# Two layers with a mixture of experts on one core: four chunks of the first expert loaded into other rooms, and another order of the experts

## The chip, the cores and the metric

The kernel runs on one core of a Trainium2 chip. The metric is the device time of one execution in microseconds, as the median over several executions. Before the change it is 1270.76 us (three runs, 1269.85 to 1271.94).

## The reference

The input x has 256 tokens (two blocks of 128) of 1024 channels, in float32. Two layers follow. Each has a token mixer made of four groups (a convolution, a pooling mixer, two kinds of attention), with one projection in (1024 to 2304) and one out (1024 to 1024). The first layer then has a dense SwiGLU of inner width 2816. The second has eight SwiGLU experts of inner width 3584, and each token goes to the two with the highest router values:

```
logits = t @ router
top_vals, top_idx = lax.top_k(logits, 2)
gates = softmax(top_vals)
combine = sum(one_hot(top_idx, 8) * gates[..., None], axis=1)
for e in range(8):
    y = y + combine[:, e:e+1] * ((silu(t @ wg[e]) * (t @ wu[e])) @ wd[e])
```

A last RMSNorm ends it. All weights are float32, and nearly all of their bytes belong to the experts.

## The kernel before

**Chunks.** The host lays all weights out as 395 chunks of 128 partitions by 2048 float32, 1 MB each (`_stream`): 13 for the mixer of layer 0, 33 for the dense network, 13 for the mixer of layer 1 (59 so far), and then 336 for the experts, 42 each. An expert is worked in seven slabs of 512 inner columns. A slab has six chunks: two for the gate, two for the up and two for the down projection. Chunk number k of an expert is numbered as they lie in memory; the kernel asks for them in the order gate and up of slab s, then down of slab s-1.

**The ring.** A chunk is loaded by `chunk` (L135; the load itself is L148), always from the queue of the engine SP, into a room of 8 KB per partition that `raw` (L125) hands out. Up to the mixer of layer 1 there are nine rooms. When that mixer's own tiles are given back, eight more rooms are laid in their place (L663), so that the experts have 17. A room is free again when the last instruction that reads it is done. The first loads of the experts are chained with `issue_after` (L147), which keeps them in program order on SP.

**High and low parts.** Where the full 128 rows of a block are multiplied, the weights are first split in two: `halves` (L167) makes, for each half of a chunk, a tile `hi` on ScalarE (L179) and a tile `lo` on VectorE (L180), 1024 elements per partition each, with four rooms for `hi` and four for `lo` (two chunks). Each product is then three matmuls (`moving`, L196).

**Wide and narrow experts.** The tokens of an expert are gathered by a one-hot matmul (`gather`, L937), turned (`gathered_T`, L947), multiplied by gate and up (`gate_or_up`, L973; the products are L208 for a wide and L991 for a narrow expert), turned again (`act_T`, L1002), multiplied by down (`down`, L1018; L208 or L1036) and scattered back (`scatter`, L1043; matmuls L1055, additions to x L1056). A wide expert has place for 128 tokens and uses the high and low parts. A narrow one has place for 64: it multiplies the chunk in float32 as it was loaded, two chains of 64 columns side by side, and doesn't touch `hi` and `lo`.

**The order of the experts.** Expert 0 comes first and is narrow; its chunks have addresses that are known when the kernel is built. The other seven are ranked by their number of tokens while the kernel runs. SP reads the seven ranks into registers (`values_load`, L1075, one after the other), because the addresses of their chunks depend on them. Ranks 0 to 2 are wide and ranks 3 to 6 narrow, and they are taken in the order of `TURNS` (L56):

```
TURNS = (0, 3, 1, 4, 2, 5, 6)
...
turns = turns + [Turn(ranked_c[r], pos_r, comb_r, r, r < WIDE) for r in TURNS]
```

So the sequence is narrow (expert 0), wide, narrow, wide, narrow, wide, narrow, narrow. Below, N0 is expert 0, N3 to N6 are the narrow ones by rank, and W0 to W2 the wide ones.

**What sets the order of each queue.** In the program text, the reading of the ranks stands ahead of all chunk loads of the experts. The stretch of the router runs under `manual_schedule`, which fixes the order on ScalarE, VectorE, GpSimd and TensorE. Everything else, SP's queue too, is laid out by the framework's planner when the kernel is built: it goes through the program by its own estimates of when operands and rooms are there, and may pull a load ahead of instructions that stand before it. On the chip each engine then takes its queue strictly in this order, and an instruction that waits holds back all that stands behind it.

Of the kernel before, what the change touches and what calls it, by code (L numbers as in the profile page):

```python
# [10 lines left out]
F32 = mybir.dt.float32  # L11
# [9 lines left out]
P = 128  # L21
# [21 lines left out]
RING = 9  # L43
RING2 = 8
LATE = 3
HALVES = 4
# [6 lines left out]


WIDE = 3
TURNS = (0, 3, 1, 4, 2, 5, 6)  # L56
NARROW = P // 2


# [34 lines left out]
def trunk(ctx: ExitStack, tc: tile.TileContext, x_in, wst, cst, par_a, par_l, gains, out):  # L94
    nc = tc.nc
# [4 lines left out]
    hi_p = ctx.enter_context(tc.tile_pool(name="hip", bufs=HALVES))  # L100
    lo_p = ctx.enter_context(tc.tile_pool(name="lop", bufs=HALVES))
# [12 lines left out]
    HF = [slice(0, 512), slice(512, 1024)]  # L114
# [8 lines left out]
    loaded = []  # L123

    def raw():  # L125
        turn[0] += 1
        return ring[(turn[0] - 1) % len(ring)].tile([P, CH], F32, name="raw")

    def gain(n, dst=None):

        g = raw()[:, :D] if dst is None else dst
        nc.sync.dma_start(g, bass.AP(tensor=gains.tensor, offset=gains.offset + n * D, ap=[[0, P], [1, D]]))
        return g

    def chunk(c, src=None, split=False):  # L135

        r = raw()
        src = wst[c] if src is None else src
        if c == 0 or split:
            for j in range(2):  # L140
                nc.sync.dma_start(r[:, j * 1024:(j + 1) * 1024], src[:, j * 1024:(j + 1) * 1024])
            if c == 0:
                nc.sync.dma_start(x[:, 1], x_in[P:, :])
        else:
            with ExitStack() as st:
                if c is not None and MOE0 < c < MOE0 + RING + RING2:
                    st.enter_context(tc.issue_after(loaded.pop()))  # L147
                loaded[:] = [nc.sync.dma_start(r, src).ins]  # L148
        return r
# [17 lines left out]
    def halves(c, on_pool=(), between=lambda: None):  # L167

        r = chunk(c) if isinstance(c, int) else c
        res = []  # L170
        for j in range(2):
            w = r[:, j * 1024:(j + 1) * 1024]
            hi = hi_p.tile([P, 1024], F32R, name="hi")
            lo = lo_p.tile([P, 1024], F32R, name="lo")
            eng = nc.gpsimd if j in on_pool else nc.vector
            with ExitStack() as st:
                for ins in behind if split[0] >= FIRST else ():
                    st.enter_context(tc.issue_after(ins))
                nc.scalar.activation(hi, w, AF.Copy)  # L179
                eng.tensor_tensor(out=lo, in0=w, in1=hi.bitcast(F32), op=SUB)  # L180
            split[0] += 1
            if split[0] == HALVES:
                behind.clear()
            res.append((hi, lo))
            if j == 0:
                between()
        return res
# [8 lines left out]
    def moving(ps, xx, w):  # L196

        return (ps, xx[0], w[0]), (ps, xx[1], w[0]), (ps, xx[0], w[1])
# [5 lines left out]
    def products(items, start=False, stop=False):  # L204

        seq = [m for it in items for m in it]
        for n, (ps, lhs, rhs) in enumerate(seq):
            nc.tensor.matmul(ps, lhs, rhs, start=start and all(m[0] is not ps for m in seq[:n]),  # L208
                             stop=stop and all(m[0] is not ps for m in seq[n + 1:]))

    def cut(pair, *at):
        return tuple(w[at] for w in pair)
# [510 lines left out]
    def moe(c0, before):  # L723
        with ExitStack() as st:
# [187 lines left out]
            class Turn:  # L912
# [5 lines left out]
                def chunk(self, k, split):  # L918
                    c = self.c + k
                    if isinstance(c, int):  # L920
                        return chunk(c, None, split)
                    return chunk(None, wst[bass.ds(c, 1)].rearrange("o p c -> (o p) c"), split)

            def experts(turns, oh=None):

                OH, XT, OT, HT, DP, adds, later = {}, {}, {}, {}, {}, {}, []
# [4 lines left out]
                ROWS = [slice(0, NARROW), slice(NARROW, P)]  # L931
# [41 lines left out]
                def gate_or_up(i, which):  # L973

                    e, s = divmod(i, NSLAB)
                    ps = acc.tile([P, 512], F32, name="acc")
                    for j in range(2):  # L980
                        r = turns[e].chunk(6 * s + 2 * which + j, False)
                        if turns[e].wide:
                            hs = halves(r)
                            for q in range(2):
                                w = tuple(h.rearrange("p (k c) -> p k c", k=2) for h in hs[q])
                                products([moving(ps, cut(XT[e], ALL, 4 * j + 2 * q + k), cut(w, ALL, k)) for k in range(2)],
                                         j + q == 0, j + q == 2)
                        else:
                            w = r.rearrange("p (k c) -> p k c", k=4)
                            for k in range(4):  # L990
                                nc.tensor.matmul(ps[ROWS[k % 2]], XT[e][:, 4 * j + k], w[:, k],  # L991
                                                 start=j == 0 and k < 2, stop=j == 1 and k > 1)
                        if later and j:
                            later.pop(0)()
                    return ps
# [22 lines left out]
                def down(i, between=()):  # L1018
                    e, s = divmod(i, NSLAB)
                    if s == 0:  # L1020
                        DP[e] = [sc.tile([P, 512], F32, name="sc") for n in range(2)]
                    for j in range(2):
                        r = turns[e].chunk(6 * s + 4 + j, i == NE * NSLAB - 1 and j == 1)
                        if turns[e].wide:
                            hs = halves(r)
                            order = [(n, hf) for n in range(2) for hf in range(2)]
                            if i == NE * NSLAB - 1 and j == 1:

                                order.sort(key=lambda o: o[1])
                            products([moving(DP[e][hf], cut(HT[i], ALL, 2 * j + n), cut(hs[n], ALL, HF[hf])) for n, hf in order],  # L1030
                                     s + j == 0, s == NSLAB - 1 and j == 1)
                        else:
                            w = r.rearrange("p (n d) -> p n d", n=2)
                            for hf in range(2):
                                for n in range(2):
                                    nc.tensor.matmul(DP[e][hf][ROWS[n]], HT[i][:, 2 * j + n], w[:, n, HF[hf]],  # L1036
                                                     start=s + j == 0, stop=s == NSLAB - 1 and j == 1)
                        for f in between if j == 0 else ():
                            f()
                    if s == NSLAB - 1:  # L1040
                        scatter(e)

                def scatter(e):  # L1043
                    ys = []
                    for hf in range(2):
                        yh = wk.tile([P, 512], F32R, name="yh", tag="hmh", bufs=2)
                        yl = wk.tile([P, 512], F32R, name="yl", tag="hml", bufs=2)
                        part(yh, yl, DP[e][hf])
                        ys.append((yh, yl))

                    def add(hf, t):
                        cc = HF[hf]
                        ps = acc.tile([P, 512], F32, name="acc") if e == NE - 1 else tr.tile([P, 512], F32, name="tr")
                        for n, y in enumerate(ys[hf]):
                            nc.tensor.matmul(ps, OT[e][:, t], y, start=n == 0, stop=n == 1)  # L1055
                        nc.vector.scalar_tensor_tensor(x[:, t, cc], ps, turns[e].weight[:, t, turns[e].col:turns[e].col + 1],  # L1056
                                                       x[:, t, cc], op0=MUL, op1=ADD)

                    for hf in range(2):
                        for t in range(NT):  # L1060
                            adds[t, hf] = lambda t=t, hf=hf: add(hf, t)
                    if e < NE - 1:
                        later.extend(adds.values())
# [8 lines left out]
                if oh is not None:  # L1072
                    weights()
                    for r in range(NE - 1):
                        v = nc.values_load(rank_i[0:1, r:r + 1], engines=[mybir.EngineType.SP], min_val=0, max_val=NE - 1)  # L1075
                        ranked_c.append(v * ECH + MOE0)
                    turns = turns + [Turn(ranked_c[r], pos_r, comb_r, r, r < WIDE) for r in TURNS]
                for i in range(NE * NSLAB):
                    e, s = divmod(i, NSLAB)
                    wide, lo = turns[e].wide, ROWS[0]  # L1080
# [174 lines left out]
```

## Time and profile before

| | |
|---|---|
| median of three runs | 1270.76 us |
| the profiled execution's own time | 1272.39 us |
| its span, from the first to the last instruction | 1270.5 us |
| mean granted clock of TensorE | 0.988 of full speed |
| TensorE busy in matmuls | 94% of the span |
| VectorE / ScalarE / GpSimd busy | 58% / 47% / 6% |
| read from the device's memory | 419.75 MB |

The profile's times count from the span's first instruction; the execution's own time holds 1.9 us more than the span. `acc`, `sc` and `tr` are accumulators of TensorE, `raw` the rooms of the ring, `wst` the stream of chunks; L208 under TensorE (PE) is a wide expert's product (or one of the mixer's), L991 and L1036 a narrow expert's.

### The profile page before, as it was taken

The page shows a single profiled execution, that of the slowest core. Times are in us where ns is not written, and L with a number is a line of the kernel's source. Part 1 is how long each engine was busy: PE and PEld are TensorE (multiplying, and loading weights), DVE is VectorE, ACT ScalarE, POOL GpSimd, SP SyncE. Part 2 cuts the span into 40 slices and gives each one's busy share as a digit, 9 for nine tenths or more (in the row PEclk, how much of TensorE's full clock was granted, in tenths as well). Part 3 has the DMA queues.
Part 4 walks back from the last instruction along what each step waited for, and adds up shares of the span by engine and source line. Part 5 has one row for each costly group of instructions (what it writes and reads, how often), then busy time and mean ns, then how long its engine had stood idle before and what let it go on. Part 6 is the DMA issues. An engine that isn't in the chain of part 4 may idle for free.

```text
span 1270.5 us, 16628 instructions
## 1 busy us (share of the span) xinstructions
PE 1198.4 (94%) x6154; PEld 791.8 (62%) x6154; DVE 738.0 (58%) x1118; ACT 596.1 (47%) x868; POOL 75.7 (6%) x45
## 2 busy tenths in 40 slices
PE   8789999999979999999999999999999999999975
PEld 6667999998767633588743378873338887333321
DVE  6986655556897521798751288883139886212112
ACT  5464544444556412576731277772137775222211
POOL 2413000001602100000000000000000000000000
PEclk9899999999999999999999999999999999999998
DMA  9523655455343499999999999999999999999994
GB/s 367 229 100 105 227 199 199 168 185 192 145 139 152 197 421 419 421 417 419 420 419 420 420 420 420 419 419 420 419 419 418 420 419 419 415 419 419 420 420 198
DMA packets 59561, 421.96 MB, mean 332 GB/s; under 512 B 6608, under 2 KB 6864, under 8 KB 9168
## 3 DMA queue, kind: packets, MB, share of 16 engines
q1 hardware_dynamic: 59472, 420.82, 81.8%
q8 instruction: 50, 0.82, 0.3%
q14 instruction: 39, 0.32, 0.1%
HBM read 419.75 MB, written 1.05 MB: 331 GB/s over the span
## 4 chain that ended last, share of the span: by engine, by line
PE 50%; DMA 11%; DVE 4%; ACT 2%; issue 1%; POOL 0%; POOLq 0%; SPq 0%; ACTq 0%; DVEq 0%
PE acc L208 17%; PE acc L991 15%; DMA raw<-wst 11%; PE sc L208 8%; PE sc L1036 5%; DVE xs L1000 1%; DVE xs L1094 1%; PE tr L942 1%; ACT xs L999 1%; PE tr L1006 1%; DVE lo L180 1%; PE tr L1055 1%; PE tr L1012 1%; PE tr L961 0%; ACT hi L179 0%
## 5 line engine op out<-in xcount | busy, mean ns | idle before, releaser
L180 DVE TENSOR_TENSOR lo<-raw,hi 128x1024 fp32r<-128x1024 f32 x351 | 419.8, 1240 | 114.7 <-ACT hi L179 110.0
L179 ACT ACTIVATE hi<-raw 128x1024 fp32r<-128x1024 f32 x370 | 374.4, 1055 | 137.7 <-PE acc L208 70.4
L991 PE MATMUL acc<-raw,xt 128*64 128x512 f32 x1120 | 251.3, 595 | 7.0 <-DMA raw<-wst 6.6
L1000 DVE TENSOR_TENSOR xs<-xs,acc 64x512 f32<-64x512 f32 x70 | 48.3, 690 | 277.6 <-ACT xs L999 277.5
L991 PEld LDWEIGHTS acc<-raw,xt 128*64 128x64 f32 x1120 | 77.3, 137 | 164.0 <-issue 143.5
L999 ACT ACTIVATE xs<-acc 64x512 f32<-64x512 f32 x70 | 41.4, 592 | 213.9 <-PE acc L991 213.9
L208 PE MATMUL acc<-lo,xgh 128*128 128x512 f32 x336 | 134.3, 400 | 1.9 <-DVE lo L180 1.6
L1036 PE MATMUL sc<-raw,ht 128*64 128x512 f32 x560 | 132.3, 598 | 2.8 <-ACT xs L999 1.9
L208 PE MATMUL acc<-hi,xgh 128*128 128x512 f32 x336 | 132.8, 395 | 0.0
L208 PE MATMUL acc<-hi,xgl 128*128 128x512 f32 x336 | 132.6, 395 | 0.0
L208 PE MATMUL sc<-hTh,hi 128*128 128x256 f32 x336 | 93.0, 277 | 0.0
L208 PE MATMUL sc<-hTl,hi 128*128 128x256 f32 x336 | 92.9, 277 | 0.0
L208 PE MATMUL sc<-hTh,lo 128*128 128x256 f32 x336 | 92.9, 276 | 0.0
L208 PE MATMUL acc<-lo,hTh 128*128 128x512 f32 (+1 forms) x192 | 71.0, 397 | 13.9 <-DVE lo L180 13.9
L1036 PEld LDWEIGHTS sc<-raw,ht 128*64 128x64 f32 x560 | 38.2, 136 | 72.5 <-issue 69.9
L208 PEld LDWEIGHTS acc<-lo,xgh 128*128 128x128 f32 x336 | 63.2, 188 | 21.3 <-DVE lo L180 6.4
L208 PEld LDWEIGHTS acc<-hi,xgl 128*128 128x128 f32 x336 | 63.2, 188 | 14.8
L208 PEld LDWEIGHTS acc<-hi,xgh 128*128 128x128 f32 x336 | 63.3, 188 | 13.8
L208 PE MATMUL acc<-hi,hTl 128*128 128x512 f32 (+1 forms) x192 | 70.5, 387 | 0.2
L208 PE MATMUL acc<-hi,hTh 128*128 128x512 f32 (+1 forms) x192 | 70.2, 393 | 0.0
L208 PE MATMUL sc<-hi,hmh 128*128 128x512 f32 x168 | 66.6, 396 | 0.0
L208 PE MATMUL sc<-hi,hml 128*128 128x512 f32 x168 | 66.4, 396 | 0.0
(265 smaller groups left out, 1550.3 us busy)
## 6 DMA issues: line engine op xcount, KB each, us to landing
raw<-wst SPq DMA_DIRECT2D x393, 1024.0 KB, 19.8
raw<-gains SPq DMA_DIRECT2D x4, 512.0 KB, 4.7
raw<-wst SPq DMA_DIRECT2D x4, 512.0 KB, 12.5
pl<-par_l SPq DMA_DIRECT2D x2, 803.5 KB, 8.8
out<-raw SPq DMA_DIRECT2D x4, 256.0 KB, 3.8
x<-x_in SPq DMA_DIRECT2D x2, 256.0 KB, 3.2
x<-x_in SPq DMA_DIRECT2D x1, 512.0 KB, 8.2
xs<-gains SPq DMA_DIRECT2D x1, 512.0 KB, 16.2
```

The source lines that it names most:

```text
L179: nc.scalar.activation(hi, w, AF.Copy)
L180: eng.tensor_tensor(out=lo, in0=w, in1=hi.bitcast(F32), op=SUB)
L208: nc.tensor.matmul(ps, lhs, rhs, start=start and all(m[0] is not ps for m in seq[:n]), stop=stop and all(m[0] is not ps for m in seq[n + 1:]))
L942: nc.tensor.matmul(pg[q].rearrange("p k c -> p (k c)"), OH[e][:, t], src[:, t, HF[q]], start=t + n == 0, stop=t + n == 2)
L991: nc.tensor.matmul(ps[ROWS[k % 2]], XT[e][:, 4 * j + k], w[:, k], start=j == 0 and k < 2, stop=j == 1 and k > 1)
L999: nc.scalar.activation(dst[ROWS[0]], ps[ROWS[0]], AF.Copy)
L1000: nc.vector.tensor_add(dst[ROWS[0]], dst[ROWS[0]], ps[ROWS[1]])
L1006: nc.tensor.transpose(ps[:, n, :NARROW], hm[ROWS[0], n * P:(n + 1) * P], ident[ROWS[0], ROWS[0]])
L1012: nc.tensor.transpose(ps[:, n], hm[:, n * P:(n + 1) * P], ident)
L1036: nc.tensor.matmul(DP[e][hf][ROWS[n]], HT[i][:, 2 * j + n], w[:, n, HF[hf]], start=s + j == 0, stop=s == NSLAB - 1 and j == 1)
L1055: nc.tensor.matmul(ps, OT[e][:, t], y, start=n == 0, stop=n == 1)
L1094: nc.vector.tensor_mul(hm[lo], hm[lo], sg[lo])
```

## The change

Three edits. `TURNS` begins with rank 3 instead of rank 0, so that the sequence is N0, N3, W0, W1, N4, W2, N5, N6. For the narrow expert with the known address (expert 0), the chunks with k from 17 to 20 are no longer loaded into the ring by `chunk` but by the new `two_tiles`: each goes as two transfers of 512 KB into one room of `hi` and one of `lo`, chained to the loads before them. In the order in which the program asks for chunks these are the 17th to 19th (k = 18, 19 and 20) and the 22nd (k = 17). And the narrow products take the half of a chunk that they need through `half`, from a chunk in one piece or from the pair of tiles.

```
-TURNS = (0, 3, 1, 4, 2, 5, 6)
+TURNS = (3, 0, 1, 4, 2, 5, 6)
...
+    def two_tiles(c):
+        r = [pool.tile([P, 1024], F32, name=n, tag=n) for pool, n in ((hi_p, "hi"), (lo_p, "lo"))]
+        for j, dst in enumerate(r):
+            with tc.issue_after(loaded.pop()):
+                loaded[:] = [nc.sync.dma_start(dst, wst[c][:, j * 1024:(j + 1) * 1024]).ins]
+        return r
+
+    def half(r, j):
+        return r[j] if isinstance(r, list) else r[:, j * 1024:(j + 1) * 1024]
...
                 def chunk(self, k, split):
                     c = self.c + k
                     if isinstance(c, int):
+                        if not self.wide and 0 <= k - RING - RING2 < HALVES:
+                            return two_tiles(c)
                         return chunk(c, None, split)
...
-                            w = r.rearrange("p (k c) -> p k c", k=4)
                             for k in range(4):
-                                nc.tensor.matmul(ps[ROWS[k % 2]], XT[e][:, 4 * j + k], w[:, k],
+                                w = half(r, k // 2).rearrange("p (k c) -> p k c", k=2)
+                                nc.tensor.matmul(ps[ROWS[k % 2]], XT[e][:, 4 * j + k], w[:, k % 2],
                                                  start=j == 0 and k < 2, stop=j == 1 and k > 1)
...
-                            w = r.rearrange("p (n d) -> p n d", n=2)
                             for hf in range(2):
                                 for n in range(2):
-                                    nc.tensor.matmul(DP[e][hf][ROWS[n]], HT[i][:, 2 * j + n], w[:, n, HF[hf]],
+                                    nc.tensor.matmul(DP[e][hf][ROWS[n]], HT[i][:, 2 * j + n], half(r, n)[:, HF[hf]],
                                                      start=s + j == 0, stop=s == NSLAB - 1 and j == 1)
```

## Rows read from the trace of the kernel before

**Rows 1.** The page: busy time of TensorE over the span, and, in 40 equal slices of the span, the share of TensorE and of the DMA engines in tenths and what the DMA engines moved.

```profile
PE 1198.4 (94%) x6154; PEld 791.8 (62%) x6154; DVE 738.0 (58%) x1118; ACT 596.1 (47%) x868; POOL 75.7 (6%) x45
...
PE   8789999999979999999999999999999999999975
...
DMA  9523655455343499999999999999999999999994
GB/s 367 229 100 105 227 199 199 168 185 192 145 139 152 197 421 419 421 417 419 420 419 420 420 420 420 419 419 420 419 419 418 420 419 419 415 419 419 420 420 198
```

**Rows 2.** Busy times of three stretches around the entry to the experts: us, busy us and instructions of each engine, TensorE's clock, the share of the DMA engines, and GB/s.

```profile
415.00:425.00 10.00, 10.00 (x49) 8.34 (x48) 4.11 (x8) 2.76 (x5) 1.40 (x2) 1.00 0.88 361
425.00:439.50 14.50, 13.39 (x91) 9.23 (x91) 10.48 (x53) 7.20 (x14) 2.11 (x2) 1.00 0.01 1
439.50:1249.50 810.00, 783.21 (x3566) 440.26 (x3564) 423.64 (x459) 371.79 (x480) 0.00 (x0) 1.00 1.01 419
```

**Rows 3.** SP's queue in order of time, 400 to 420 us and 436 to 446 us: start, length, number of loads. It issued nothing between the two.

```profile
402.07 12.64 SPq L148 DMA_DIRECT2D raw<-wst  x8
...
438.84 6.88 SPq L148 DMA_DIRECT2D raw<-wst  x9
```

**Rows 4.** What SP's queue waited for, in 427 to 436 us (first row) and in 1040 to 1100 us (second): us in total, times, the longest.

```profile
SPq L1075 <- DVE by_rank L851: 20.0, 1, 20.0
...
SPq L148 <- DVE lo L180: 27.9, 11, 4.8
```

**Rows 5.** VectorE's last step before the ranks can be read, from the timeline.

```profile
434.44 0.22 DVE L851 TENSOR_TENSOR by_rank<-cs,rf 128x64 bf16<-128x64 f32 x1
```

**Rows 6.** Chunk loads issued from SP: number, size and median us from issue to landing. First from the start to 427 us (two rows: whole chunks, and the first chunk in two pieces), then from 436 to 439 us, from 1075 to 1080 us, and over the whole span (the page).

```profile
raw<-wst SPq DMA_DIRECT2D x71, 1024.0 KB, 4.9
raw<-wst SPq DMA_DIRECT2D x2, 512.0 KB, 7.0
...
raw<-wst SPq DMA_DIRECT2D x1, 1024.0 KB, 4.8
...
raw<-wst SPq DMA_DIRECT2D x2, 1024.0 KB, 10.3
...
raw<-wst SPq DMA_DIRECT2D x393, 1024.0 KB, 19.8
```

**Rows 7.** The chain that ended last, in order of time (start, us, what): the last products of the mixer's projection out, and then the first and last products of the experts. L991 begins a narrow expert, L208 after L1036 begins a wide one, L1036 x24 ends a narrow one. The last two rows are the last load of the stream and the products on it.

```profile
414.93 6.64 PE acc L208 x29
...
422.45 2.75 PE acc L208 x12
...
436.55 10.52 PE acc L991 x48
...
512.90 5.33 PE sc L1036 x24
...
522.13 12.95 PE acc L208 x54
...
628.30 0.02 issue
...
631.18 2.59 PE acc L208 x10
...
646.22 1.87 PE acc L991 x8
...
736.56 12.96 PE acc L208 x54
...
860.74 1.87 PE acc L991 x8
...
951.07 12.99 PE acc L208 x54
...
1075.20 1.87 PE acc L991 x8
...
1231.23 19.84 DMA raw<-wst
...
1251.21 4.38 PE sc L1036 x16
```

**Rows 8.** Busy times by stretch (columns as in rows 2), from the first product of one expert to that of the next: W0, N3, and N5; the last row runs from the first product of N6 to the last.

```profile
522.13:646.22 124.09, 124.00 (x552) 99.52 (x554) 105.80 (x101) 88.85 (x100) 0.00 (x0) 1.00 1.01 419
646.22:736.56 90.34, 85.56 (x399) 30.25 (x399) 24.40 (x37) 23.42 (x41) 0.00 (x0) 1.00 1.01 419
...
1075.20:1161.60 86.40, 83.02 (x394) 28.94 (x393) 19.43 (x28) 19.57 (x36) 0.00 (x0) 1.00 1.01 418
1161.60:1255.59 93.99, 82.69 (x371) 25.89 (x370) 17.95 (x26) 16.08 (x30) 0.00 (x0) 1.00 0.97 400
```

**Rows 9.** VectorE's instructions by group in the stretch of N3 (646 to 736 us), those that hand one expert over to the next: shapes, number, busy us, mean ns, idle time before them.

```profile
L1056 DVE SCALAR_TENSOR_TENSOR x<-tr,comb_r,x 128x512 f32<-128x512 f32 x6 | 4.4, 748 | 3.9 <-PE tr L1055 3.8
L216 DVE TENSOR_TENSOR yl<-sc,yh 128x512 fp32r<-128x512 f32 x4 | 2.7, 689 | 6.2 <-ACT yh L215 6.2
L216 DVE TENSOR_TENSOR xgl<-tr,xgh 128x512 fp32r<-128x512 f32 x2 | 1.3, 686 | 1.8 <-ACT xgh L215 1.8
```

**Rows 10.** TensorE in order of time near the end (start, us, products, and in brackets the idle time before them and what ended it).

```profile
1208.72 1.94 PE L991 MATMUL acc<-raw,xt 128*64 128x512 f32 x8 [1.04 <-DMA raw<-wst]
1211.21 1.94 PE L991 MATMUL acc<-raw,xt 128*64 128x512 f32 x8 [0.56 <-DMA raw<-wst]
```

## The prediction

> **What bounds the kernel now.** Begin with the page's 40 slices [rows 1]: from the fifteenth slice (445 us) to the end TensorE, the DMA engines and the rate of some 420 GB/s all stand at their top together. That is the experts' part, and its share of busy time doesn't say which of the two sets the end. The stretches say more [rows 2]: from 439.5 to 1249.5 us the DMA engines never stop, 419 GB/s or 2.50 us for a chunk of 1.0486 MB; but from 425 to 439.5 they move nothing. Why is seen on SP's queue [rows 3]: eight loads between 402 and 415 us, then none until 438.84, when nine go out in 7 us. SP was waiting 20.0 us for `by_rank` [rows 4], which is done at 434.66 [rows 5], and then spent 4.2 us on reading seven ranks. Up to 427 us 71 whole chunks and one in two pieces were issued [rows 6], 72 in all; 59 belong to the earlier stages, so 13 chunks of N0 were ahead of the ranks on SP, not the 17 that have rooms.
>
> Now the boundaries of the experts on the chain [rows 7]. Loads first: the 14th chunk is issued at 438.84 and lands 4.8 us later [rows 6], at 443.6; the 336th lands at 1251.07 (1231.23 + 19.84). Between lie 322 chunks and the final gain of half a chunk: 807.4 / 322.5 = 2.504 us each. So chunk n lands at 443.6 + 2.504 (n - 14) as long as SP isn't held up. Uses: N0 ends at 518.2 (42 used, 43.8 landed), W0 begins at 522.13, N3 at 646.22, W1 at 736.56, N4 at 860.74, W2 at 951.07, N5 at 1075.20. From one start to the next a wide expert takes 124.1 us, and TensorE is busy in 124.00 of them; a narrow one takes 90.3 ahead of a wide and 86.4 ahead of a narrow one [rows 8]. The loads of one expert take 42 x 2.504 = 105.2 us. So each narrow expert eats into the stock of landed chunks and each wide one builds it up again, and the old order alternates. TensorE first waits for a load at 1207.7 us, in N6 [rows 10]; until then the products set the pace, after it the loads do.
>
> **The change, step by step.**
>
> *The early loads.* Their rooms of `hi` and `lo` are last read by the products that end at 425.2 us [rows 7], while the DMA engines fall idle at about 424.5, so the rooms are there in time. The queue is not. The new loads are chained behind the 16 that stand ahead of them, and three of these 16 (14th to 16th) already go out behind the reading of the ranks. Nothing that the planner sees before that point is altered by the diff. I therefore take it that SP's queue stays as it is up to there, and that the four chunks go out after 438.84, where the DMA engines are full anyway. Gain: 0; bound, if all are pulled ahead: the hole of 15.0 us (424.5 to 439.5) is filled and every landing is 15 us earlier.
>
> *Eight half transfers for four whole ones.* Four more issues on SP, of 0.4 us each by the burst of nine in 6.88 us where it had some waits [rows 3], beside transfers in flight. A load takes 19.8 us to land over most of the span [rows 6], eight times 2.5, so eight are in flight; with halves that is 4 MB or 10 us of work, and at 10.3 us to landing (1075 us) the engines were still full [rows 6, 8]. I take 0. Below nothing isn't possible, since the bytes are the same; the other bound is that each extra transfer costs what a lone one takes over the steady pace, 4.8 - 2.5 = 2.3 us, 9.2 us for four. The Trainium skill, in "DMA: Bandwidth & Descriptors", section "Bandwidth", speaks against such halves: it advises transfers of at least 1 MiB. With its fixed 2.0 us for each transfer (section "Anatomy of one DMA — SWDGE (gpsimd) path") the four extra ones would add 8 us to the loads, as an estimate; here the row of 19.8 us shows these times lying on top of each other.
>
> *The products of N0.* As many matmuls of the same shapes, from two tiles instead of one: 0. Reads from other rooms have no price in this trace; the products of wide experts read the same rooms at full pace, so I bound it by 0.
>
> *N3 second.* This is the term that decides. N0 ends at 518.2 with 1.8 chunks in stock. Undelayed, N3 would end 86.4 us later, at 604.6; but its last chunk, the 84th, lands at 443.6 + 70 x 2.504 = 618.9. So N3 is paced by the loads, as N6 is now. Its last eight products (1.87 us) end at 620.8. The hand-over to a wide expert then takes what it took after N0, 522.13 - 518.23 = 3.9 us, so W0 starts at 624.7.
>
> *W0 and W1 back to back.* W0 takes 124.1. A wide expert behind a wide one isn't in the trace. Added on VectorE at that place are two `yl` (0.69 us), two `xgl` (0.69) and four additions to x (0.75) [rows 9], 5.7 us; VectorE is free for 18.3 of 124.1 us in a wide expert [rows 8]. Bounds: 0 (all lies in its free time) and 5.7 us (all of it delays `lo`). I take 3 us, by the nearest row: TensorE's pause of 2.9 us at the gather in W0's last slab (628.30 to 631.18) [rows 7]. W1 starts at 624.7 + 124.1 + 3 = 751.8, N4 at 875.9, W2 at 966.2, N5 at 1090.3: 15.1 us later than now.
>
> *The ring runs full.* With loads unhindered, 14 + (1090.3 - 443.6) / 2.504 = 272.3 chunks would have landed by then, 20.3 more than the 252 used. Now, at 1075.2, it is 266.2, or 14.2 ahead, with 10.3 us to landing, which is 4.1 in flight: 18.3 together, and SP already waits for rooms (`lo`) there [rows 4]. Without a loss there must be about as many in flight as a lone landing time of 4.8 us covers, 1.9; so at most 16.4 can be ahead. The other 3.9 chunks are 9.8 us in which the DMA engines stand still. Bounds: with 0 in flight, 18.3 ahead and 5.0 us; with the 4.1 of today, 14.2 ahead and 15.3 us. I take 9.8.
>
> *The end.* At 1090.3 there are 268.4 landed; 67.6 and the half for the gain are left, 68.1 x 2.504 = 170.5 us. The last lands at 1260.8, and the last products come 4.5 us behind it as now (1255.59 - 1251.07) [rows 7]: 1265.3 against 1255.6, **+9.7 us**. TensorE alone would need 1090.3 + 86.4 + 81.7 (N0's length) = 1258.4, so the loads bind, narrowly. What follows the last product is unchanged. The sum is made against the profiled execution (span 1270.5, time 1272.39), which lies 1.6 us over the median; on the median it gives 1270.8 + 9.7 = **1280.5 us**. With the bounds of the hand-over (-3 to +2.7) and of the ring (-4.8 to +5.5, not below TensorE's +2.8) its own range is 1275 to 1287, the ends of both not added up.
>
> **Rivals.**
>
> *It does what it says (1265.5).* The planner pulls the new loads, and those before them, ahead of the ranks. For it: their rooms are free by 425 us. Against it: three loads with rooms stand behind the ranks now. Then landings are 15 us earlier: chunk 84 at 603.9, N3's end at 605.8, W0 at 609.7, W1 at 736.8, N4 at 860.9, W2 at 951.2, N5 at 1075.3, as now. Stock is 3.9 chunks over the limit as above; from there 170.5 + 4.5 give 1250.3, -5.3 us. This is the side of "faster"; it decides as soon as at least six chunks (15 us) more go out before 434 us.
>
> *The full ring costs little (1275.7).* Loads keep pace down to none in flight: 5.0 us lost instead of 9.8, +4.9. For it: at 4.1 in flight nothing was lost. Against: a lone load takes 4.8 us.
>
> *The wide hand-over is dear (1283.2).* All 5.7 us of VectorE's work are exposed, +2.7 on the forecast. For it: ScalarE and VectorE take their queues in order, as the 2.9 us pause shows. Against: 18.3 us of free time.
>
> *The halves break up the stream (1289.7).* +9.2 us ahead of N3, whose end the loads set. Against it: eight in flight.
>
> *No difference (1270.8).* N3's wait is all made good in N6, which waits for loads today, and the ring doesn't fill. Against it: the stock of 20.3 chunks has no rooms, and TensorE alone ends 2.8 us later.
>
> **How the numbers follow.** Chances: forecast 0.52; does what it says 0.11; ring costs little 0.17; dear hand-over 0.12; halves 0.03; no difference 0.05. A difference under 0.2% (2.5 us) can't be told from none. All but two cases are slower: slower 0.84, same 0.05, faster 0.11. The range 1273 to 1287 leaves out the first rival, the halves and no difference, 0.19; the forecast's own range, 1275 to 1287, lies in it.
>
> **What would show it.** SP's queue: one gap from about 415 to 438.8 us, with the pairs of 512 KB behind it, and the DMA engines idle from 425 to 439.5. TensorE waiting for `raw` loads in N3 from some 540 us on, and W0's first product at 625 rather than 609. N5's first product near 1090. SP's waits for `lo` at the end of W1 and W2 longer than 4.8 us, and the DMA share below 1 there. The prediction is wrong if 512 KB loads are issued before 434 us, or if N3 ends by 606 us.

## The result and the profile after

The changed kernel takes 1282.87 us (median of four runs, 1282.34 to 1284.99) against 1270.55 (four runs of the kernel before): 1.0101 times the time before, with a 95% interval of 1.0089 to 1.0113. Forecast was 1280.5, slower. The profiled execution has a span of 1280.8 us and a time of 1282.63.

The page's slices, as in [rows 1]:

```profile
PE   8789999999889999878999999999999999999985
...
DMA  9533555455344499999999999999999999999995
GB/s 367 225 99 128 214 191 194 179 198 190 115 165 190 195 419 420 419 419 421 418 420 419 419 420 419 415 361 362 419 420 418 420 420 397 390 419 419 420 419 217
```

Three things are to be seen. The hole before the fifteenth slice is still there. TensorE falls to 8, 7 and 8 in the 17th to 19th slices, which is N3. And two new dents stand in the GB/s, 361 and 362 near 850 us and 397 and 390 near 1080 us.

The hole first. SP's queue in order of time around the reading of the ranks, as [rows 3], and its wait there, as [rows 4] (the line of the reading is now L1087, that of a chunk load L159, of the halves L140):

```profile
399.95 12.64 SPq L159 DMA_DIRECT2D raw<-wst  x8
...
436.73 1.28 SPq L159 DMA_DIRECT2D raw<-wst  x3
438.10 0.60 SPq L140 DMA_DIRECT2D hi<-wst  x1
438.80 0.40 SPq L140 DMA_DIRECT2D lo<-wst  x1
439.28 0.41 SPq L140 DMA_DIRECT2D hi<-wst  x1
439.78 0.47 SPq L140 DMA_DIRECT2D lo<-wst  x1
...
SPq L1087 <- DVE by_rank L862: 20.0, 1, 20.0
```

Eight loads, the same 20.0 us for the ranks, then three chunks, and only then the pairs of halves. "Loaded early" did not happen.

N3 next: TensorE in order of time, its idle time and what ended it in brackets.

```profile
523.72 1.94 PE L1004 MATMUL acc<-raw,xt 128*64 128x512 f32 x8 [0.54 <-DMA raw<-wst]
526.21 1.94 PE L1004 MATMUL acc<-raw,xt 128*64 128x512 f32 x8 [0.56 <-DMA raw<-wst]
...
548.66 1.94 PE L1004 MATMUL acc<-raw,xt 128*64 128x512 f32 x8 [0.56 <-DMA raw<-wst]
...
556.13 1.94 PE L1004 MATMUL acc<-raw,xt 128*64 128x512 f32 x8 [0.56 <-DMA raw<-wst]
```

Eight products take 1.94 us and begin every 2.5 us, the time of one load: N3 goes at the pace of the loads, as the end of N6 did before [rows 10].

And the dents: busy times by stretch (columns as in [rows 2]) at the end of W1 and of W2, and what SP waited for from 820 to 900 us.

```profile
840.00:850.00 10.00, 10.00 (x47) 8.15 (x46) 9.49 (x10) 7.47 (x9) 0.00 (x0) 1.00 0.97 382
850.00:860.00 10.00, 9.89 (x43) 7.72 (x42) 6.49 (x8) 6.78 (x9) 0.00 (x0) 1.00 0.88 327
860.00:870.00 10.00, 10.00 (x52) 7.94 (x51) 8.31 (x10) 6.66 (x9) 0.00 (x0) 1.00 0.93 351
870.00:880.00 10.00, 10.00 (x42) 5.13 (x42) 5.11 (x7) 2.52 (x4) 0.00 (x0) 1.00 0.88 324
...
1080.00:1090.00 10.00, 10.00 (x50) 6.99 (x48) 6.48 (x8) 5.09 (x7) 0.00 (x0) 1.00 0.97 362
1090.00:1100.00 10.00, 9.58 (x43) 3.20 (x40) 4.69 (x7) 1.81 (x3) 0.00 (x0) 1.00 0.95 357
...
SPq L159 <- DVE lo L191: 43.6, 17, 4.8
```

TensorE is full while the loads fall to 324 GB/s, and SP waits for `lo`, which is what frees a room of the ring in a wide expert. The kernel before at the same places, and SP's wait there from 820 to 900 us:

```profile
820.00:900.00 80.00, 78.55 (x358) 44.97 (x358) 43.53 (x48) 36.23 (x48) 0.00 (x0) 1.00 1.01 420
...
1080.00:1090.00 10.00, 9.58 (x45) 3.41 (x46) 4.32 (x6) 2.56 (x5) 0.00 (x0) 1.00 1.01 402
...
SPq L148 <- DVE lo L180: 15.0, 6, 3.1
```

There the loads keep their pace. The 402 is the only stretch of ten microseconds under 417 GB/s, with the DMA engines' share at 1.01, and the chunks land every 2.5 us all through it (1085.09, 1087.54, 1090.03). SP waited for `lo` before too, but 6 times and not 17.

The boundaries on the chain, as in [rows 7] (L1004 and L1048 are a narrow expert's products, L219 a wide one's):

```profile
434.40 10.52 PE acc L1004 x48
...
618.48 1.96 PE sc L1048 x8
...
624.35 12.96 PE acc L219 x54
...
748.45 3.25 PE acc L219 x14
...
874.08 1.87 PE acc L1004 x8
...
964.42 12.99 PE acc L219 x54
...
1088.65 1.87 PE acc L1004 x8
...
1241.24 19.86 DMA raw<-wst
...
1261.24 4.37 PE sc L1048 x16
```

One thing has to be set straight before the numbers are compared. The stages ahead of the experts end at another time in each profiled execution: N0's first product came at 436.55 us in the one of before and at 434.40 in this one, and between 432.5 and 437.4 in all of this study. So lengths are counted from N0's first product to the last product of N6: 819.0 us before (1255.58 - 436.55) and 831.2 after (1265.61 - 434.40), 12.2 us more, which agrees with the medians.

### The profile page after: what moved, and what is told of

Same layout as the page of the kernel before. It is cut to its first block, busy times and chain, and to the rows that moved or that the text cites. A ratio compares the mean times of both kernels' runs of the same rounds, so it can differ in the third digit from the quotient of the medians.

```text
span 1280.8 us, 16638 instructions
## 1 busy us (share of the span) xinstructions
PE 1200.7 (94%) x6154; PEld 788.3 (62%) x6154; DVE 735.6 (57%) x1118; ACT 595.3 (46%) x868; POOL 74.3 (6%) x45
## 4 chain that ended last, share of the span: by engine, by line
PE 45%; DMA 18%; DVE 3%; ACT 1%; issue 1%; POOL 0%; POOLq 0%; SPq 0%; ACTq 0%; DVEq 0%
PE acc L219 19%; DMA raw<-wst 18%; PE acc L1004 9%; PE sc L219 9%; PE sc L1048 3%; PE tr L955 1%; PE tr L1025 1%; DVE xs L1013 1%; PE tr L1067 1%; DVE xs L1106 1%; ACT xs L1012 1%; PE tr L1019 1%; DVE lo L191 0%; ACT hi L190 0%; DVE raw L915 0%
## 5 line engine op out<-in xcount | busy, mean ns | idle before, releaser
L191 DVE TENSOR_TENSOR lo<-raw,hi 128x1024 fp32r<-128x1024 f32 x351 | 420.0, 1240 | 112.7 <-ACT hi L190 107.7
L1004 PE MATMUL acc<-raw,xt 128*64 128x512 f32 x1096 | 249.1, 597 | 15.7 <-DMA raw<-wst 15.2
L1004 PEld LDWEIGHTS acc<-raw,xt 128*64 128x64 f32 x1096 | 74.0, 136 | 175.9 <-issue 129.5
L1048 PE MATMUL sc<-raw,ht 128*64 128x512 f32 x552 | 131.3, 599 | 6.6 <-ACT xs L1012 4.5
L219 PE MATMUL acc<-lo,xgh 128*128 128x512 f32 x336 | 134.1, 399 | 1.4 <-DVE lo L191 1.1
L219 PE MATMUL acc<-hi,xgh 128*128 128x512 f32 x336 | 132.8, 395 | 0.0
L219 PE MATMUL acc<-hi,xgl 128*128 128x512 f32 x336 | 132.6, 395 | 0.0
L219 PE MATMUL sc<-hTh,hi 128*128 128x256 f32 x336 | 93.0, 277 | 0.0
L219 PE MATMUL sc<-hTl,hi 128*128 128x256 f32 x336 | 92.8, 276 | 0.0
L219 PE MATMUL sc<-hTh,lo 128*128 128x256 f32 x336 | 92.8, 276 | 0.0
L1048 PEld LDWEIGHTS sc<-raw,ht 128*64 128x64 f32 x552 | 37.3, 136 | 77.2 <-issue 69.4
L219 PE MATMUL acc<-lo,hTh 128*128 128x512 f32 (+1 forms) x192 | 69.0, 385 | 10.5 <-DVE lo L191 10.5
L219 PEld LDWEIGHTS acc<-lo,xgh 128*128 128x128 f32 x336 | 63.2, 188 | 20.1 <-DVE lo L191 5.2
L219 PEld LDWEIGHTS acc<-hi,xgl 128*128 128x128 f32 x336 | 63.2, 188 | 14.8
L219 PEld LDWEIGHTS acc<-hi,xgh 128*128 128x128 f32 x336 | 63.3, 188 | 14.0
L219 PE MATMUL acc<-hi,hTh 128*128 128x512 f32 (+1 forms) x192 | 70.5, 396 | 0.0
L219 PE MATMUL acc<-hi,hTl 128*128 128x512 f32 (+1 forms) x192 | 70.0, 385 | 0.2
L219 PE MATMUL sc<-hi,hmh 128*128 128x512 f32 x168 | 66.6, 396 | 0.0
L219 PE MATMUL sc<-hi,hml 128*128 128x512 f32 x168 | 66.5, 396 | 0.0
```

The source lines that it names most:

```text
L1048: nc.tensor.matmul(DP[e][hf][ROWS[n]], HT[i][:, 2 * j + n], half(r, n)[:, HF[hf]], start=s + j == 0, stop=s == NSLAB - 1 and j == 1)
```

## The experiments

All ratios are to the kernel before, taken on the same chip. "Length" is the stretch just named, from the profile. A table of all comes at the end of this part.

**The order alone.** The kernel before with one line changed:

```
-TURNS = (0, 3, 1, 4, 2, 5, 6)
+TURNS = (3, 0, 1, 4, 2, 5, 6)
```

> The kernel before with the new order of experts alone (rank 3 ahead of rank 0), no loads into the rooms of hi and lo. Theory (the order makes the whole loss, because the second narrow expert waits for its chunks and the two wide ones in a row fill the ring): the time of the changed kernel, 1282 to 1284 us. Rival (part of the loss comes from the eight half transfers or from products that read other rooms): 1274 to 1281 us.

1282.9 us, 1.0085 (1.0069 to 1.0100). Nearly the whole loss is the order's: its length is 829.9 us, 10.9 of the 12.2.

**The rooms alone.** The changed kernel with the old order:

```
-TURNS = (3, 0, 1, 4, 2, 5, 6)
+TURNS = (0, 3, 1, 4, 2, 5, 6)
```

> The changed kernel with the old order of experts: only the four chunks in the rooms of hi and lo. Theory (they go out behind the reading of the ranks, when the DMA engines are full anyway): no difference, 1269.5 to 1271.5 us. Rival one (the halves break up the stream of loads): 1273 us or more. Rival two (they do come early and help): 1267 us or less.

1272.16 us, 1.0005 (0.9996 to 1.0015): no difference that can be told from none. The median is 0.7 us over the range given; the kernel before stood at 1271.29 beside it. Length 819.6, +0.6. The half transfers show no cost, and the early rooms give nothing, because the loads that should use them stand behind the ranks.

**The ranks read late.** The changed kernel, with the reading of the ranks moved in the program and tied behind the load of k = 17:

```
-                    for r in range(NE - 1):
-                        v = nc.values_load(rank_i[0:1, r:r + 1], ...)
-                        ranked_c.append(v * ECH + MOE0)
-                    turns = turns + [Turn(...) for r in TURNS]
...
                         down(i - 1, (lambda: act_T(i),) if s == NSLAB - 1 else ())
+                    if i == 3 and oh is not None:
+                        with tc.issue_after(loaded[0]):
+                            for r in range(NE - 1):
+                                v = nc.values_load(rank_i[0:1, r:r + 1], ...)
+                                ranked_c.append(v * ECH + MOE0)
+                        turns = turns + [Turn(...) for r in TURNS]
```

> The changed kernel with the reading of the ranks moved on SP behind the loads of the first 22 chunks, so that these can go out as soon as their rooms are free. Theory (SP, held up by the ranks, keeps the DMA engines idle from 425 to 438 us; filled, every landing is about 15 us earlier, the second narrow expert doesn't wait for its last chunk, and what is left of the loss is the full ring at the end of the wide experts): the hole is gone from the DMA share, the first product of a wide expert comes near 608 us and the time is 1264 to 1269 us. Rival (the hole isn't SP's, the rooms aren't free before the first products): the hole stays and the time is about 1282 us.

1266.32 us, 0.9957 (0.9943 to 0.9970). SP's queue in order of time, then busy times around the entry (columns as in [rows 2]), and the first product of W0 and what follows, from the chain:

```profile
402.97 14.04 SPq L159 DMA_DIRECT2D raw<-wst  x11
420.88 0.33 SPq L140 DMA_DIRECT2D hi<-wst  x1
421.31 0.38 SPq L140 DMA_DIRECT2D lo<-wst  x1
...
429.37 0.33 SPq L140 DMA_DIRECT2D lo<-wst  x1
```

```profile
425.00:439.00 14.00, 12.90 (x89) 9.55 (x89) 10.92 (x53) 7.20 (x14) 2.94 (x2) 1.00 1.00 397
...
820.00:900.00 80.00, 78.57 (x358) 44.80 (x358) 43.09 (x48) 35.73 (x47) 0.00 (x0) 1.00 0.95 374
...
1060.00:1110.00 50.00, 48.66 (x228) 23.23 (x229) 21.84 (x26) 15.94 (x24) 0.00 (x0) 1.00 0.96 383
```

Eleven loads in place of eight, then the halves as their rooms come free, from 420.88 us on: the stretch of the hole now moves 397 GB/s. So in the changed kernel the wait at the ranks made the hole, not the rooms. W0's first product comes 173.1 us after N0's (610.50 - 437.41) instead of 190.0, so the wait in N3 is all but gone: TensorE waits for loads there 4 times, 1.7 us in all, where it was 22 times and 11.9 us. The dents at the end of W1 and W2 are still there (374 and 383 GB/s).

**A wide and a narrow in turn, behind two narrow ones.** The kernel before, again one line:

```
-TURNS = (0, 3, 1, 4, 2, 5, 6)
+TURNS = (3, 0, 4, 1, 5, 2, 6)
```

> The kernel before with the order N0, N3, W0, N4, W1, N5, W2, N6: a second narrow expert first, then wide and narrow in turn; nothing else. It has the wait in N3 but no two wide experts in a row. Theory (of the 12 us some 4 come from the wait in N3, the rest from the full ring at the end of W1 and W2): no stretch with a DMA share under 0.97, TensorE alone sets the end, +3.7 us: 1273 to 1276 us. Rival (the wait in N3 is the whole loss): 1281 to 1284 us.

1277.88 us, 1.0048 (1.0032 to 1.0063): a miss by 2 us on the upper side, and 3 us under the rival. The end shows why it isn't the changed kernel's loss. Its busy times from 600 to 1240 us, and TensorE in order of time at the end:

```profile
600.00:1240.00 640.00, 624.91 (x2824) 386.66 (x2824) 388.83 (x407) 335.01 (x414) 0.00 (x0) 1.00 1.01 419
```

```profile
1246.50 5.75 PE L991 MATMUL acc<-raw,xt 128*64 128x512 f32 x26
1252.08 1.89 PE L1036 MATMUL sc<-raw,ht 128*64 128x512 f32 x8
```

Share 1.01 and 419 GB/s all through: the ring holds nothing up. And no wait for `raw` at the end: TensorE's own work sets it. Length 824.7, +5.7. So the wait in N3 costs 5.7 us of the length, and this is net: it delays W0 by 16.5 us (189.1 us after N0, against 172.6 in the run below that has this order, the rooms and the ranks read late), but the kernel before waits for loads in N6 instead, which takes 93.99 us there [rows 8] and 82.5 here. Two wide experts in a row add 5.2 us (829.9 with the order alone), net again: the ring holds up the loads, and the end waits for them once more.

**One room less.** The changed kernel with 16 rooms in the ring:

```
-RING2 = 8
+RING2 = 7
```

> The changed kernel with one room less in the ring (16 instead of 17). Theory (the ring is full at the end of W1 and W2, and the stock held there is what the rest of the stream starts from): one chunk time more, 2.5 us, so 1285 to 1286 us. Rival (the DMA share under 1 at these places is from something else, such as SP's waits or the hand-over): 1282 to 1283.5 us as in the changed kernel.

1286.8 us, 1.0119 (1.0103 to 1.0134). The medians lie 3.9 us above the changed kernel's and the ratios 2.3 us, and the two intervals overlap, so this run alone doesn't settle it. The profile is sharper, since the two wide experts end at the same place (N5's first product 654.2 us after N0's in both): from there to the last product it takes 179.2 us, where it was 176.95 with 17 rooms. One room is worth 2.2 us, close to one load of 2.50. The edit does one more thing: the same constant sets which chunks go into `hi` and `lo`, now k = 16 to 19, and the common place of N5 shows no price of that up to there. Counted load by load in the traces, N5's first product finds 15 chunks landed and 2 in flight in the changed kernel, 14 and 2 here: in both as many as there are rooms.

**Ranks late in the old order.** The same move of the reading in the kernel before.

> The kernel before with the reading of the ranks moved on SP behind the loads of the first 22 chunks; old order, no loads into other rooms. Theory (with the old order the stock of landed chunks at the end of the last wide expert is held to some 15.5 by the ring, and it is 14.2 today, so early loads can't be kept until they are needed): 1266 to 1269 us, with a DMA share under 1 around 860 and 1075 us. Rival (loads bind from end to end, and each us of the filled hole comes off the time): 1256 to 1261 us.

1265.6 us, 0.9956 (0.9941 to 0.9971), by the length 3.8 us less. The range given was missed by under a us, the rival by more than four. The hole was half filled (229 GB/s in 425 to 439 us), and the ring now holds up the loads at the ends of W1 and W2, which it did not before: busy times there,

```profile
820.00:900.00 80.00, 78.56 (x359) 43.77 (x357) 41.74 (x48) 34.55 (x46) 0.00 (x0) 1.00 0.99 398
...
1060.00:1110.00 50.00, 48.66 (x229) 22.21 (x229) 19.80 (x24) 14.06 (x23) 0.00 (x0) 1.00 0.98 386
```

**All three together, and without the rooms.** The order narrow, narrow, then wide and narrow in turn, with the ranks read late; once with the four chunks in the rooms of `hi` and `lo`, once without.

> The changed kernel with the ranks read late and the order N0, N3, W0, N4, W1, N5, W2, N6. Theory (the early chunks carry the two narrow experts, the stock stays between none and 13, so neither a wait for loads nor a full ring is left and TensorE alone sets the end, 10 us earlier than in the kernel before): 1259 to 1262 us, no DMA share under 0.97 before the last 20 us. Rival (what the hole gives is lost again elsewhere, as in the changed order with late ranks): 1265 us or more.

1262.22 us, 0.9929 (0.9915 to 0.9942): a little over the range given, but by the length 10.7 us less, as reckoned. (The stages ahead vary by some us, which can make up the difference; that it does is not shown.) It beats both kernels.

```profile
425.00:439.00 14.00, 12.89 (x72) 6.53 (x74) 7.81 (x45) 7.28 (x11) 0.04 (x1) 1.00 1.01 408
...
820.00:900.00 80.00, 80.00 (x355) 64.57 (x354) 71.03 (x68) 58.92 (x65) 0.00 (x0) 1.00 1.01 419
1060.00:1110.00 50.00, 50.00 (x221) 40.47 (x220) 43.41 (x42) 38.75 (x42) 0.00 (x0) 1.00 1.01 419
```

No hole, no dent.

> As the run with the late ranks and the order N0, N3, W0, N4, W1, N5, W2, N6, but without the four chunks in the rooms of hi and lo. Theory (17 rooms are full at about 435 us, the next load must wait for the first products, so some 3 to 4 us of the hole stay and the second narrow expert ends that much later): 1262 to 1266 us, 3 to 4 us slower than with the rooms. Rival (the rooms of hi and lo give nothing once the ranks are read late): the same time as with the rooms.

1267.7 us, 0.9964 (0.9950 to 0.9977), over the range given: the rooms do more than I said. They are worth 6.8 us of the length (815.1 against 808.3), twice the 3 to 4 expected: 252 GB/s in 425 to 439 us instead of 408, and W0 begins 179.4 us after N0 instead of 172.6. The landings say why it is twice as much. Without the rooms no chunk lands between 434.8 and 442.8 us, and none between 450.3 and 454.0, 5.5 and 1.3 us over the pace of 2.50; with them there is no such gap. The expectation has the wait for a room, but not the time that a load issued alone then takes to land, 4.9 us. So the early loads are sound in this order; they lacked a queue that lets them act.

The lengths, worked out from the profiles (us; the last two columns are counted from N0's first product, and from the first product behind the last wide expert to the last product):

| run | N0 begins at | length | to W0 | behind the last wide one |
|---|---|---|---|---|
| before | 436.55 | 819.0 | 85.6 | 180.4 |
| after | 434.40 | 831.2 | 190.0 | 177.0 |
| order alone | 436.38 | 829.9 | 189.1 | 176.4 |
| rooms alone | 433.45 | 819.6 | 85.6 | 181.0 |
| after, ranks late | 437.41 | 814.4 | 173.1 | 177.0 |
| in turn | 435.51 | 824.7 | 189.1 | 82.5 (N6 only) |
| after, 16 rooms | 435.48 | 833.4 | 189.9 | 179.2 |
| before, ranks late | 433.82 | 815.3 | 85.6 | 176.5 |
| in turn, ranks late, rooms | 432.54 | 808.3 | 172.6 | 82.6 (N6 only) |
| in turn, ranks late | 435.94 | 815.1 | 179.4 | 82.5 (N6 only) |

The last column shows the ring's rule. Where two narrow experts follow the last wide one and the ring of 17 rooms has held up the loads, the rest takes 176.4 to 177.0 us whatever came before. Worked back as in the prediction, at its pace: (176.95 - 4.5) / 2.504 - 0.5 = 68.4 chunks are still to land, so 336 - 68.4 - 252 = 15.6 are held. In the kernel before it was 14.2, and the rest took 180.4. What the traces show when the chunks are counted one by one follows in the next part.

## Why the prediction was right

The order of events was right, and the sum came out 2.5 us short of the 12.2 in the profile.

*The early loads give nothing.* Right: SP's queue kept its order up to the ranks, the hole stayed, and the rooms alone made no difference. That the wait at the ranks is the cause was argued before and is now shown by the run in which they are read late.

*Half transfers cost nothing.* Right within what can be told: 1.0005, +0.6 us of length. The larger price of 9.2 us is excluded. Nor did the 8 us show that the prediction works out from the Trainium skill ("DMA: Bandwidth & Descriptors", section "Anatomy of one DMA — SWDGE (gpsimd) path"); that section is on transfers issued from GpSimd, and these are issued from SP.

*N3 is paced by the loads.* Right. W0's first product was forecast 188.15 us after N0's (624.7 - 436.55); it came after 189.95. With the order alone it is 189.1. So the halves may account for 0.85 of the 1.8 us, but that is a difference of single profiles; the rest is mostly the interpolated landing of chunk 84, forecast 182.35 us after N0's first product and 183.2 with the order alone. N3's first wait came earlier than said, at 523 us instead of 540. The stock of 1.8 chunks was an average: it says when loads and products cross, not when a single chunk is first late.

*W0 and W1 back to back.* The 3 us for the hand-over were too much. W0 to W1 took 124.10 (748.45 - 624.35), which is nothing over a wide expert's own time, and W1 125.63, so the additions to x and the rest cost 1.5 us in all, spread over the first slabs of W1. The lower of my two bounds was nearly it.

*The ring runs full.* The mechanism was right, the size off by 2 us. A reading was wrong to begin with: the load that lands at 1251.07 in the kernel before [rows 7] is the 335th chunk; the last one goes in two pieces and lands at 1253.60. So the line of landings stands too high at N5's first product, 266.2 where 265 are counted, and the 18.3 chunks that the sum has there, landed or in flight, are more than the 17 rooms. Counted, it is 13 landed and 4 in flight before the change, and 15 and 2 in the changed kernel, with the order alone, with the ranks read late, and with the ranks late in the old order. All rooms are taken in each; what differs is how many of them hold a load that is still on its way. So 1.9 in flight was right for that place.

What failed is the step behind it. I took it that 1.9 loads in flight suffice to keep the engines at their pace, because a lone load lands in 4.8 us. The row that shows otherwise, loads issued from 870 to 875 us in the changed kernel:

```profile
raw<-wst SPq DMA_DIRECT2D x1, 1024.0 KB, 5.6
```

At 5.6 us to landing, 2.2 in flight by my measure, the engines moved only 324 GB/s. At N5 the same holds. From the last landing ahead of its first product, the next eight chunks take 23.0 us in the changed kernel, and 20.0 in the kernel before, where 4 are in flight. A part of these 3 us comes back, since the stock at that point is half a chunk larger than forecast (2.7 chunks more than before, with the share of the chunk on its way, where I said 16.4 - 14.2 = 2.2). About 2 us are left. I also counted the loss once, at the end of W2; it falls mostly at the end of W1 (the dents from 830 to 900 us), and the limit is met a second time at W2. The sum doesn't care, because the limit at W2's end alone sets what is left to load. One of the signs named did not come: SP's waits for `lo` at the ends of W1 and W2 are more, but none is longer than 4.8 us.

*The terms together.* From N0's first product to N5's, 653.75 us were forecast and 654.25 measured: +1.8 in N3 and -1.5 in the hand-over nearly cancel, which is luck. From N5 to the end, 175.0 forecast and 176.95 measured. That is the 2.5 us.

*The rivals.* "It does what it says" was put at 1265.5; what it described is the run with the late ranks, 1266.3. "The full ring costs little" falls with the dents, the run with 16 rooms and the 176.95 us behind N5 (it needs 170.2), "the hand-over is dear" with 124.10, "no difference" with the result.

## What to carry to other kernels

A load is only as early as the place of its issue in its queue: before giving it a room, look at what the issuing engine waits for ahead of it, here 20 us for seven numbers that are not needed before the 43rd load goes out, some 60 us later (it lands at 443.6 + 29 x 2.504 = 516.2, issued 19.8 us before). Where stages in turn use up and build up a stock of loaded data, keep the account at each boundary (loaded less used, against the rooms): an order that ends one stretch with none and another with more than fits loses on both, however full the engines look on average. With the queue cleared and the experts in turn, the same rooms were worth 7 us and the kernel came out 0.7% under its old time: that order keeps the stock within the rooms.

## What the runs showed of the hardware

The stream of 1 MB loads needs four of them in flight here to keep its 419 GB/s, not the two that a lone load's 4.8 us to landing would suggest. Counted from issue to landing over the experts' part (450 to 1235 us), in the five runs whose ring holds up the loads (the changed kernel, the order alone, 16 rooms, and the ranks read late in the changed and in the old order), the engines move 418 to 421 GB/s in the stretches with four in flight, 391 to 401 with three, and 341 to 362 with two; each figure rests on 44 to 64 us. And the point at which the experts begin moved by 3.1 us between profiled executions of kernels that are the same up to there (433.45 us in the run with the rooms alone, 436.55 before the change). The shift is there already at SP's eight loads around 400 us (399.00 against 402.07); why was not looked into.
